# A streaming encoder step in one scheduled stream: first queries in ring tiles, gate products by the memory branch, and the end of attention

## The chip, the cores and the metric

One core of one Trainium2 chip runs the whole program. The metric is the device time of one execution in microseconds (us), lower is better. The engines have short names: PE is the matmul engine TensorE, PEld its weight loads, DVE VectorE, ACT ScalarE, POOL GpSimd, and SP the engine whose queue issues the DMAs. Each engine works off its own queue in order and waits at semaphores for the others.

## The reference

One layer of an encoder on 1024 prompt tokens and 64 sample tokens, in fp32. The three branches of the mixer and the three gates come out of one projection:

```python
h = rmsnorm(x, g_mix); p = h @ w_in
qa, ka, va, qi, ki, wi, ub, qm, gates = split(p)
a = dsa_attend(...)        # 8 query heads on 2 kv heads of 64, over keys that an indexer selects per query
b = pool_mix(ub)           # trailing means over 2, 4, 8, 16 tokens, and a linear map per group
m = memory_attend(qm, mk, mv)   # 4 heads of 128, 256 memory tokens
ga, gb, gm = sigmoid(gates)
x = x + (ga * (a @ w_oa) + gb * (b @ w_ob) + gm * (m @ w_om)) @ w_out
y = x + (silu(h2 @ w_gate) * (h2 @ w_up)) @ w_down      # h2 = rmsnorm(x)
```

## The kernel before, in words

Every fp32 product is made of three matmuls of rounded halves, high by high, high by low and low by high (`matmul3`, L118); a half is made by a rounding copy (`whi` by L98 on POOL, `ph` by L799 on ACT) and a subtraction on DVE (`lo_of`, L88). The kernel is one program text that the Tile framework's scheduler turns into one queue per engine, at build time. What sets the order there is the program's data, the tiles' rings (a tile name with a tag and `bufs=n` has n buffers, handed out in the order of the program text, and a later one waits until the buffer's last reader is done) and explicit `issue_after` marks; independent matmuls are drawn between others.

Around the change the work runs in this order. The keys and values are projected token block by token block (L124, `mm<-tmhi,hh`): a block is normed and rotated (L216 on ACT, L127 and L128 on POOL, L220 and L154 to L157 on DVE), the keys are split (`kd`, L592, L593), transposed (L599), copied (L602) and stored to `k_t` in HBM (L603). The memory cross-attention comes next, in two halves of two heads. In each, the memory keys are transposed (L753); for each of eight blocks of 128 tokens the queries are loaded (`qn`, L758), transposed (L761), split (`qh` L779, `ql` L780), multiplied with the keys (`mm<-kh,qh`), softmaxed (maximum L727 on DVE, exponentials L732 on ACT, reciprocal L733, two scalings L735 on POOL), transposed again (L741), split (`ph` L799, `pl` L88), and multiplied with the values for two blocks together (`mm<-ph,vh`), whose result is split into `bh` and `bl` (L810, L88).

Beside this runs `fill_gate(0, side_a[:, 0], 0, 8)`: the eight 128-column blocks of the gate of branch a, f = 0 to 7. Each loads a raw weight tile (`fraw`), splits it into a pair of tiles `whi` and `wlo` (rings of two buffers each), and multiplies it in three chunks of 364, 362 and 362 tokens with the normed input's halves `hh` and `hl`: 72 matmuls with names like `fl<-hh,whi`, a tanh (L247, `fsg`) per chunk and a store (L635). These products need nothing of the branches. After the memory branch stand the products of its result with w_om (`fill_om`, `fl<-bh,whi`), whose ready-made halves are loaded into the same `whi` and `wlo` rings from `w_pre`.

Then the queries of attention's first block are loaded (`q0`, a tile of the ring `raw` of three buffers, which also holds the memory branch's keys and values), split (`qs0`, L870 and L871), transposed (L883) and copied (`qT_first`, L884). Attention works off blocks of 128 queries in the order `BLOCKS = (2, 7, 1, 6, 0, 8, 5, 4, 3)`, for two key heads each: logits (L1053), mask and maximum (L1065), exponentials (L1067), reciprocal (L1069), scalings (L1071, four on POOL), transposes (L1085), split into `ph` (L1089) and `pl` (L88), value products (L1093), then the result's parts (L1098 to L1102) and its halves (L1111, L1112). The values are split once by `split_values` (L1014, L1015). The last step (block 3, key head 1) has nothing after it but the merge: `merge` (L1150 and following) multiplies the result with w_oa, and L1159 and L1160 combine it with the gate on DVE. Four merges of the first 384 tokens stand in the attention's end (`tr<-bh,whi`); the loop after it takes all other chunks (`mm<-bh,whi`, 352 wide).

## Time and profile before

| | us |
|---|---|
| median of 3 runs | 1708.93 (1707.88 to 1710.14) |
| the profiled execution | 1706.33 |
| its span on the core | 1704.6 |
| PE busy | 1678.4 |
| DVE busy | 1136.4 |
| ACT busy | 808.3 |
| POOL busy | 410.2 |
| DMA, mean | 169 GB/s |

The profiled execution's own time is 1.7 us longer than its span. Busy times are sums over instructions; for PE, matmuls overlap and their ends are modelled, so a busy PE isn't PE at its peak. A wait in the profile names the instruction that released the waiting one. The granted clock is a share of TensorE's full speed.

### The profile page before, as it was taken

The page shows a single profiled execution, that of the slowest core. Times are in us where ns is not written, and L with a number is a line of the kernel's source. Part 1 is how long each engine was busy: PE and PEld are TensorE (multiplying, and loading weights), DVE is VectorE, ACT ScalarE, POOL GpSimd, SP SyncE. Part 2 cuts the span into 40 slices and gives each one's busy share as a digit, 9 for nine tenths or more (in the row PEclk, how much of TensorE's full clock was granted, in tenths as well). Part 3 has the DMA queues.
Part 4 walks back from the last instruction along what each step waited for, and adds up shares of the span by engine and source line. Part 5 has one row for each costly group of instructions (what it writes and reads, how often), then busy time and mean ns, then how long its engine had stood idle before and what let it go on. Part 6 is the DMA issues. An engine that isn't in the chain of part 4 may idle for free.

```text
span 1704.6 us, 32578 instructions
## 1 busy us (share of the span) xinstructions
PE 1678.4 (98%) x12037; PEld 1635.4 (96%) x12037; DVE 1136.4 (67%) x2552; ACT 808.3 (47%) x1942; POOL 410.2 (24%) x480
## 2 busy tenths in 40 slices
PE   9999999999999997999999999999999999999999
PEld 8999999999999997889898999999999999999999
DVE  7578999999973433767673676667657565575543
ACT  5456667755723444776532443334334333353331
POOL 4212424434431223553403431111111000000000
PEclk9999999999999999999999999999999999999999
DMA  6455851234365237435677634554535443596761
GB/s 226 135 181 204 280 158 47 73 129 146 118 217 162 87 102 243 127 119 170 215 266 257 196 117 133 195 195 149 188 113 182 146 170 103 177 368 220 213 189 54
DMA packets 158383, 288.61 MB, mean 169 GB/s; under 512 B 18184, under 2 KB 95872, under 8 KB 158224
## 3 DMA queue, kind: packets, MB, share of 16 engines
q1 hardware_dynamic: 158224, 286.53, 50.6%
q8 instruction: 95, 1.56, 0.4%
q14 instruction: 64, 0.52, 0.1%
HBM read 194.60 MB, written 91.87 MB: 168 GB/s over the span
## 4 chain that ended last, share of the span: by engine, by line
PE 55%; DVE 1%; ACT 1%; issue 0%; POOL 0%; DVEq 0%; ACTq 0%
PE mm L1370 25%; PE mm L1597 14%; PE mm L124 11%; PE fl L124 2%; PE acc L1093 1%; PE tr L1053 1%; PE mm L1085 1%; DVE pl L88 0%; POOL pr L1071 0%; ACT pr L1067 0%; ACT ph L1089 0%; PE mm L1308 0%; DVE pr L1065 0%; PE tr L124 0%; PE tr L1031 0%
## 5 line engine op out<-in xcount | busy, mean ns | idle before, releaser
L1370 PE MATMUL mm<-hi,whi 128*128 128x288 f32 (+1 forms) x1120 | 322.9, 289 | 1.1 <-ACT whi L1362 1.1
L1370 PE MATMUL mm<-lo,whi 128*128 128x288 f32 (+1 forms) x1120 | 323.4, 289 | 0.0
L1370 PE MATMUL mm<-hi,wlo 128*128 128x288 f32 (+1 forms) x1120 | 323.3, 290 | 0.0
L1370 PEld LDWEIGHTS mm<-hi,whi 128*128 128x128 f32 x1120 | 211.8, 189 | 1.6 <-ACT whi L1362 1.6
L1370 PEld LDWEIGHTS mm<-lo,whi 128*128 128x128 f32 x1120 | 211.7, 189 | 0.0
L1370 PEld LDWEIGHTS mm<-hi,wlo 128*128 128x128 f32 x1120 | 211.0, 189 | 0.0
L124 PE MATMUL fl<-hh,whi 128*128 128x362 f32 (+1 forms) x528 | 174.5, 330 | 0.0
L124 PE MATMUL fl<-hl,whi 128*128 128x362 f32 (+1 forms) x528 | 174.3, 330 | 0.0
L124 PE MATMUL fl<-hh,wlo 128*128 128x362 f32 (+1 forms) x528 | 173.8, 329 | 0.0
L1597 PE MATMUL mm<-ul,wh 128*128 128x256 f32 (+1 forms) x600 | 171.7, 288 | 0.0
L1597 PE MATMUL mm<-uh,wh 128*128 128x256 f32 (+1 forms) x600 | 171.1, 288 | 0.0
L1597 PE MATMUL mm<-uh,wl 128*128 128x256 f32 (+1 forms) x600 | 170.3, 288 | 0.0
L921 ACT ACTIVATE junk_a<-score,cand_a,sgn_a 128x512 f16<-128x512 f32 (+2 forms) x93 | 95.5, 1027 | 45.8 <-DVE cand_a L938 21.1
L1597 PEld LDWEIGHTS mm<-ul,wh 128*128 128x128 f32 x600 | 112.7, 188 | 0.0
L1597 PEld LDWEIGHTS mm<-uh,wh 128*128 128x128 f32 x600 | 112.4, 188 | 0.0
L1597 PEld LDWEIGHTS mm<-uh,wl 128*128 128x128 f32 x600 | 112.2, 188 | 0.0
L124 PEld LDWEIGHTS fl<-hh,whi 128*128 128x128 f32 x528 | 99.3, 188 | 0.7
L124 PEld LDWEIGHTS fl<-hh,wlo 128*128 128x128 f32 x528 | 99.3, 188 | 0.6
L124 PEld LDWEIGHTS fl<-hl,whi 128*128 128x128 f32 x528 | 99.3, 188 | 0.4
L88 DVE TENSOR_TENSOR wl<-raw,wh 128x512 fp32r<-128x512 f32 x75 | 51.8, 690 | 70.6 <-ACT wh L1587 70.5
L924 DVE TENSOR_SCALAR_CACHE_REDUCE junk_v<-score,cand_v 64x192 f16<-64x192 f32 (+1 forms) x124 | 93.9, 757 | 2.6
L1587 ACT CAST wh<-raw 128x512 fp32r<-128x512 f32 x75 | 46.6, 621 | 101.1 <-PE mm L1597 97.8
(447 smaller groups left out, 4638.3 us busy)
## 6 DMA issues: line engine op xcount, KB each, us to landing
uf<-u SPq DMA_DIRECT2D x75, 272.0 KB, 4.1
raw<-in_w_up_dram SPq DMA_DIRECT2D x26, 512.0 KB, 3.9
fraw<-in_w_gates_dram SPq DMA_DIRECT2D x23, 512.0 KB, 4.1
fr<-in_w_gate_dram SPq DMA_DIRECT2D x22, 512.0 KB, 4.0
dr<-in_w_down_dram SPq DMA_DIRECT2D x22, 512.0 KB, 6.0
s<-dr SPq DMA_DIRECT2D x22, 512.0 KB, 2.9
raw<-s SPq DMA_DIRECT2D x44, 256.0 KB, 4.0
whi<-w_pre SPq DMA_DIRECT2D x20, 512.0 KB, 4.0
```

What stands on the lines that cost most here:

```text
L88: return V.tensor_tensor(lo, src, hi.bitcast(F32), op=OP.subtract)
L124: PE.matmul(ps, l, r, start=i == 0, stop=i == len(prods) - 1)
L921: A.activation(junk[:n, :nk], sc, AF.Sign, bias=bj, scale=1.0 if scale is None else scale[:n, j:j + 1], accum_out=sj)
L924: V.tensor_scalar(junk[:n, :nk], sc, bj, None, op0=OP.is_ge, op1=OP.add, accum_out=sj)
L1053: lm = PE.matmul(lg[:n, i * 512:i * 512 + cn], qT[:, h, :n], kT[:, kv, s, k0 + c:k0 + c + cn], start=s == 0, stop=s == 1)
L1085: t_ = PE.transpose(pt[:cn, i * n:(i + 1) * n], probs[i][:, c:c + cn], ident[:n, :n])
L1093: m_ = PE.matmul(acc, vv, r, start=ji == 0 and i == 0, stop=ji == nj - 1 and i == 1)
L1370: PE.matmul(dst[i], l, r, start=start and j == 0, stop=stop and j == 11, skip_group_check=True)
L1587: A.copy(wh, raw)
L1597: PE.matmul(acc[f, i], l[:, fs], r[:, cs], start=start and j == 0, stop=stop and j == 2, skip_group_check=True)
```

## The change

It makes these edits:

1. The first queries' code (load, split, transposes, copies) moves in the text from behind `fill_gate(0, ...)` to ahead of it. `qT_first` takes a buffer of the ring `raw`, and `qs0` one of the ring `whi`, where both had a pool of their own.
2. `matmul3` returns its last matmul. For the last gate block (f = 7) the second and third chunk are issued after the memory branch's last value product. `split_values` is issued after the last copy into `qT_first`.
3. In the last softmax (block 3, key head 1) DVE doubles the sums, and ACT takes the scalings of every second head, so that POOL has two and not four.
4. The halves of the last block's first key head are made with POOL and no longer with DVE (L1112).
5. For the third and fourth merge in attention's end, DVE's two operations are issued after the last `pl`.
6. The merge loop's first block takes the tokens from 736 ahead of those from 384.

```diff
-    def fill_gate(base, dst, f0=0, f1=KT):
+    def fill_gate(base, dst, f0=0, f1=KT, last=None):
         for f in range(f0, f1):
             w = fgate(base + f)
             for c0, cn in CH:
-                SP.dma_start(dst[f, :, c0:c0 + cn], fsig(w, c0, cn))
+                with tc.issue_after(last) if last and f == f1 - 1 and c0 else nullcontext():
+                    sg = fsig(w, c0, cn)
+                SP.dma_start(dst[f, :, c0:c0 + cn], sg)
...
-    rest = [(f, ci) for f in range(KT) for ci in (1, 0)]
-    fill_gate(0, side_a[:, 0], 0, 8)
-    for _ in range(1):
-        fill_om(*rest.pop(0))
...
-    early_c = tc.tile_pool(name="early", bufs=1)
-    early = early_c.__enter__()
-    qT_first = early.tile([128, HA, 128], F32R, name="qT0")
+    qT_first = wp.tile([128, 1024], F32R, name="qT0", tag="raw", bufs=3).rearrange("p (h t) -> p h t", h=HA)
     q0 = raw_tile()[:, :512].rearrange("p (h d) -> p h d", h=HA)
     SP.dma_start(q0.rearrange("p h d -> p (h d)"), q_a[TS[BLOCKS[0]][0]:TS[BLOCKS[0]][0] + 128])
-    qs0 = early.tile([128, HA, 2, HDA], F32R, name="qs0")
+    qs0 = wl.tile([128, 1024], F32R, name="qs0", tag="whi", bufs=2).rearrange("p (h s d) -> p h s d", h=HA, s=2)
...
-        A.copy(qT_first[:, g:g + 4], ps.rearrange("p (h t) -> p h t", h=4))
+        qt_copy = A.copy(qT_first[:, g:g + 4], ps.rearrange("p (h t) -> p h t", h=4)).ins
+
+    rest = [(f, ci) for f in range(KT) for ci in (1, 0)]
+    fill_gate(0, side_a[:, 0], 0, 8, mem_mm[0])
+    for _ in range(1):
+        fill_om(*rest.pop(0))
...
+                end = (b, kv) == (BLOCKS[-1], 1)
+                if end:
+                    V.tensor_scalar(sm, sm, 2.0, None, op0=OP.mult)
                 V.reciprocal(sm, sm)
                 for j, pr in enumerate(probs):
-                    G.tensor_scalar(pr, pr, sm[:, j:j + 1], 0.5, op0=OP.mult, op1=OP.mult)
+                    if end and j % 2:
+                        A.activation(pr, pr, AF.Copy, scale=sm[:, j:j + 1])
+                    else:
+                        G.tensor_scalar(pr, pr, sm[:, j:j + 1], 1.0 if end else 0.5, op0=OP.mult, op1=OP.mult)
...
-                    halves_of(av, cs, t0, n, V if b == BLOCKS[-1] else G)
+                    halves_of(av, cs, t0, n, V if (b, kv) == (BLOCKS[-1], 1) else G)
...
                 if not todo:
-                    split_values()
+                    with tc.issue_after(qt_copy):
+                        split_values()
...
-        V.scalar_tensor_tensor(gt, gt, 1.0, ps, op0=OP.add, op1=OP.mult)
-        V.tensor_tensor(pin, pin, gt, op=OP.add)
+        with tc.issue_after(last_pl[0]) if after and f > 1 else nullcontext():
+            V.scalar_tensor_tensor(gt, gt, 1.0, ps, op0=OP.add, op1=OP.mult)
+            V.tensor_tensor(pin, pin, gt, op=OP.add)
...
-        for c0, cn in ACH[1:]:
+        for c0, cn in ACH[1:] if f else ACH[:0:-1]:
```

The order of the instructions shows what the scheduler makes of it. On PE, where the key projection ends and the memory branch begins (`kd` are the split keys, `raw` the memory keys, `qn` the branch's queries), before:

```order
L124 MATMUL fl<-hh,whi 128x364
L599 MATMUL mm<-ident_r,kd 128x64
L753 MATMUL mm<-ident,raw 128x128 x2
L599 MATMUL mm<-ident_r,kd 128x64 x3
L753 MATMUL mm<-ident,raw 128x128 x2
L124 MATMUL fl<-hl,whi 128x364
L124 MATMUL fl<-hh,wlo 128x364
L124 MATMUL fl<-hh,whi 128x362
```

And in the changed program, from the last projection matmul to the first logits (`mm<-kh,qh`; its line numbers are 1 to 4 higher):

```order
L124 MATMUL mm<-tmhi,hl 64x256
L600 MATMUL mm<-ident_r,kd 128x128 x4
L600 MATMUL mm<-ident_r,kd 128x64
L757 MATMUL mm<-ident,raw 128x128 x4
L600 MATMUL mm<-ident_r,kd 128x64 x3
L765 MATMUL mm<-ident,qn 128x128 x4
L124 MATMUL mm<-kh,qh 128x256
L124 MATMUL mm<-kl,qh 128x256
L757 MATMUL mm<-ident,raw 128x128 x4
```

Before, 42 gate matmuls stand between the last two blocks' key transposes, and 46 between L753 and the first query transposes (L761). Now no gate product of f = 0 to 7 stands in the key projection or in the branch's first half: the first of them follows 196 matmuls after the first query transpose, in the second half. Those of f = 0 and 1 are spread over the second half, and those of f = 2 to 7, with the last of f = 1, stand in one piece of 426 behind the branch's last value product. The query transposes of attention's first block (L883, now L873) stand shortly ahead of that piece, and before they stood behind all gate products. From the second `fill_om` product on, PE's order is the same up to the end of attention.

On SP, in the second half of the memory branch, the load of attention's first queries (`raw<-q_a`) and what stands around it, before (`fraw` is a gate's raw weights, `fsg` a gate's result):

```order
L747 DMA raw<-in_cache_mem_k_dram 128x2x256
L635 DMA side_a<-fsg 128x364
L635 DMA side_a<-fsg 128x362 x2
L749 DMA raw<-in_cache_mem_v_dram 128x2x256
L758 DMA qn<-q_m 128x256
L113 DMA fraw<-in_w_gates_dram 128x1024
L758 DMA qn<-q_m 64x256
L635 DMA side_a<-fsg 128x364
L877 DMA raw<-q_a 128x512
```

And in the changed program:

```order
L751 DMA raw<-in_cache_mem_k_dram 128x2x256
L753 DMA raw<-in_cache_mem_v_dram 128x2x256
L762 DMA qn<-q_m 128x256
L762 DMA qn<-q_m 64x256
L762 DMA qn<-q_m 128x256
L867 DMA raw<-q_a 128x512
L762 DMA qn<-q_m 128x256 x2
L113 DMA fraw<-in_w_gates_dram 128x1024
L762 DMA qn<-q_m 128x256
L638 DMA side_a<-fsg 128x364
```

The load of the first queries keeps its place behind the second half's memory tiles, since it takes a buffer of their ring. The tile `qs0` now precedes the gates in the ring of `whi`, and the gates' weight loads and stores have moved behind it.

On DVE, at the end of attention (`pl` are the low halves of the probabilities, `gt<-gt,tr` the merges of the first 384 tokens, `bl<-ot,bh` the last block's low halves), before:

```order
L88 TENSOR_TENSOR pl<-mm,ph 128x512
L88 TENSOR_TENSOR pl<-fl,ph 128x512
L1112 TENSOR_TENSOR bl<-ot,bh 128x2x128
L1159 SCALAR_TENSOR_TENSOR gt<-gt,tr 128x384
L1160 TENSOR_TENSOR gt<-gt 128x384
L88 TENSOR_TENSOR pl<-mm,ph 128x512
L1233 MEMSET ones 128x128
L1101 TENSOR_TENSOR ot<-acc,ot 64x256
```

And in the changed program:

```order
L88 TENSOR_TENSOR pl<-mm,ph 128x512
L88 TENSOR_TENSOR pl<-fl,ph 128x512
L88 TENSOR_TENSOR pl<-mm,ph 128x512
L1168 SCALAR_TENSOR_TENSOR gt<-gt,tr 128x384
L1169 TENSOR_TENSOR gt<-gt 128x384
L1242 MEMSET ones 128x128
L1109 TENSOR_TENSOR ot<-acc,ot 64x256
```

The last three low halves now follow each other, with the third merge's two operations behind them; L1112 of the first key head has left DVE.

## The prediction

> **What bounds the kernel now.** I read four views: the busy table of the page, the waits of TensorE (PE), the windows that cut the span into stretches, and the timeline. The busy table says that there is almost nothing to win on PE's side:

> ```profile
> PE 1678.4 (98%) x12037; PEld 1635.4 (96%) x12037; DVE 1136.4 (67%) x2552; ACT 808.3 (47%) x1942; POOL 410.2 (24%) x480
> ```

> PE is idle for 1704.6 - 1678.4 = 26.2 us in all, and every matmul of the program is still there after the change. So an edit can gain only what PE waits, and loses as much as PE newly waits. The change touches two places. In the first, from the key and value projection to the first attention logits, the waits of PE (480 to 660 us: us in total, times, longest) are:

> ```profile
> PE fl L124 <- ACT qT L884: 4.2, 1, 4.2
> PE mm L883 <- DVE qs L871: 2.1, 1, 2.1
> PE mm L599 <- ACT kd L592: 0.5, 1, 0.5
> ```

> The windows (columns: width, busy us with instructions of PE, PEld, DVE, ACT, POOL, then granted clock, DMA share, GB/s) show the same place from the projection's end to the first queries:

> ```profile
> 518.00:526.00 8.00, 8.00 (x57) 8.00 (x55) 3.13 (x7) 2.22 (x9) 1.93 (x3) 1.00 0.34 100
> 526.00:534.00 8.00, 8.00 (x50) 7.52 (x50) 1.19 (x3) 2.33 (x5) 0.00 (x0) 1.00 0.59 173
> 560.00:600.00 40.00, 40.00 (x279) 39.70 (x278) 17.57 (x35) 17.64 (x48) 6.76 (x12) 1.00 0.29 93
> 600.00:640.00 40.00, 40.00 (x269) 38.74 (x268) 15.09 (x35) 16.67 (x51) 8.58 (x15) 1.00 0.29 92
> ...
> 650.00:655.00 5.00, 2.91 (x23) 2.55 (x22) 2.70 (x5) 1.10 (x2) 1.01 (x1) 1.00 0.59 187
> 655.00:660.00 5.00, 0.82 (x6) 0.68 (x5) 0.00 (x0) 3.39 (x11) 3.39 (x7) 0.73 0.98 327
> 660.00:665.00 5.00, 5.00 (x19) 5.00 (x19) 0.56 (x1) 0.00 (x0) 2.23 (x4) 0.59 1.06 382
> 665.00:670.00 5.00, 5.00 (x31) 5.00 (x30) 1.58 (x4) 0.71 (x2) 2.57 (x3) 1.00 0.70 230
> ```

> Two things are to be seen. Around 655 us PE stands still while the first queries are split, transposed and copied, and behind it the clock is low. But from 518 to 640 us, where short chains run over four engines, PE is never idle. What keeps it busy there are the gate products (`fl<-hh,whi`), long runs of matmuls that wait for nothing; the order of the changed program takes them away from exactly there, because the first queries' tile now stands ahead of them in the ring of two `whi` tiles, and its load stands behind the raw tiles of the memory branch's second half.

> **The change part by part. First queries, gain.** The two waits go, since the gate products of f=2 to 7 now stand behind the query transposes: 4.2 + 2.1 = 6.3 us. The low clock behind them goes too: 31 matmuls in 665 to 670 against 19 in 660 to 665, 12 fewer at 5.00 / 31 = 0.16 us, 1.9 us. What is late next is the weight pair of the first product behind the gates:

> ```profile
> whi<-w_pre SPq DMA_DIRECT2D x20, 512.0 KB, 4.0
> ```

> Its load stands on SP between the stores of the last gate's second and third chunk, so only one chunk of 24 matmuls (24 x 0.16 = 3.9 us) and not all of the tanh, store and 4.0 us of landing is covered: I take 0.9 us of new wait (0 to 2.5). Gain 6.3 + 1.9 - 0.9 = 7.3 us (5.7 to 8.2). ACT's and POOL's splitting of the values (L1014, L1015) moves behind the gates' tanh, but the chain to the first scaled probabilities is longer than it; I cost it at nothing, and the rivals have its price. On SP, the gates' stores and weight loads go from between the branch's loads to behind them, and the value loads (`vf`) stand behind the last gate's stores. That the last gate's last two products wait for the branch's last values costs nothing: their whole group now stands behind it anyway.

> **Lost cover, projection of keys and values.** Timeline rows, one block's last projection matmul and the end of its chain (squares, norm, rotary, split `kd`), then the last block's:

> ```profile
> 502.26 0.28 PE L124 MATMUL mm<-tmhi,hl 128*128 128x256 f32 x1
> 506.10 0.33 PE L124 MATMUL mm<-tmhi,hh 128*128 128x256 f32 x1
> 506.18 0.42 DVE L593 TENSOR_TENSOR kd<-qr,kd 128x256 fp32r<-128x256 f32 x1 [0.47 <-ACT kd L592]
> 509.18 0.28 PE L124 MATMUL mm<-tmhi,hl 128*128 128x256 f32 x1
> ...
> 519.84 0.28 PE L124 MATMUL mm<-tmhi,hl 128*64 128x256 f32 x1
> 519.96 0.46 PE L599 MATMUL mm<-ident_r,kd 128*128 128x128 f32 x4
> 523.75 1.05 POOL L98 TENSOR_SCALAR whi<-fraw 128x1024 fp32r<-128x1024 f32 x1 [1.46 <-PE fl L124]
> 523.99 1.08 DVE L593 TENSOR_TENSOR kd<-qr,kd 64x256 fp32r<-64x256 f32 x1 [0.47 <-ACT kd L592]
> ```

> The chain takes 506.60 - 502.54 = 4.1 us. Now only the next block's 24 matmuls lie over it, 509.46 - 506.10 less the transposes' 0.46 = 2.9 us, so a block can be short by 1.2; but a wait gives the following chain a head start, so that two neighbours together are short of at least 4.1 - 2.9 - 0.46 = 0.7 and at most twice that: between 0.35 and 0.75 a block, 0.55 for some four blocks, 2.2 us (0.5 to 4). The last block has no successor: 525.07 - 520.12 = 4.95, less 0.46 of transposes, is 4.5. In it the split took 1.08 us on half the rows beside POOL's gate split, against 0.42 on its own; that gate split is gone, so I take 4.95 - 0.66 - 0.46 = 3.8 (2.5 to 4.5).

> [...]

> **Lost cover, start of the memory branch.** Timeline rows, the branch's wait on SP's queue (526 to 536 us), and the line view of the query load:

> ```profile
> 528.31 0.44 PE L753 MATMUL mm<-ident,raw 128*128 128x128 f32 x2
> 529.26 0.56 SPq L603 DMA_DIRECT2D k_t<-kt  x1
> 532.18 0.80 SPq L758 DMA_DIRECT2D qn<-q_m  x2
> 536.68 0.86 ACT L779 ACTIVATE qh<-mm,gqm_c 128x256 fp32r<-128x256 f32 x2 [2.81 <-PE mm L761]
> 537.19 0.88 DVE L780 SCALAR_TENSOR_TENSOR ql<-mm,gqm_c,qh 128x256 fp32r<-128x256 f32 x2 [2.89 <-ACT qh L779]
> ```
> ```profile
> SPq L758 <- DMA k_t<-kt: 1.6, 1, 1.6
> ```
> ```profile
> DMA to landing us min/median/max: 2.0/2.5/5.1
> ```

> The first queries of the branch cannot be loaded until the last key store has landed, and the store comes after the last transposes. From PE's last transpose, 528.75, to the second load's issue, 532.98, and its landing at 2.5 are 6.7 us; 46 gate matmuls filled them before, and nothing does now. Less the 0.2 by which the store is earlier without gate traffic ahead, 6.5 us (5.5 to 7.5). Then the queries' split into `qh` and `ql`, each half of its pair's 0.86 and 0.88, lies bare before the first logits: 0.9 us (0.5 to 1.5).

> **Lost cover, the branch's first half.** Timeline rows of one chunk (128 tokens, two heads), then two rows of the lines grouped by form:

> ```profile
> 540.96 0.28 PE L124 MATMUL mm<-kl,qh 128*128 128x256 f32 x1
> 541.08 0.28 PE L124 MATMUL mm<-kh,ql 128*128 128x256 f32 x1
> ...
> 544.07 0.94 POOL L735 TENSOR_SCALAR ex<-ex,sm 128x256 f32<-128x256 f32 x2 [5.57 <-DVE mx L728]
> ```
> ```profile
> L88 DVE TENSOR_TENSOR pl<-mm,ph 128x512 fp32r<-128x512 f32 x16 | 10.9, 689 | 1.9 <-ACT ph L799 1.9
> ...
> L799 ACT CAST ph<-mm 128x512 fp32r<-128x512 f32 x16 | 9.2, 588 | 8.5 <-PE mm L741 8.5
> ```

> From a chunk's last logit (541.36) to its scaled probabilities (545.01) are 3.65 us. PE has two later chunks' logits ahead of the transposes, 12 x 0.12, and 0.5 of query transposes: 1.9. So the first chunk waits 1.7. From then on the value products lie in between, but they wait for `ph` and `pl`, 0.588 + 0.689 = 1.3, with about 0.3 of transposes over it: 1.0 for each of four pairs, 4.0. For queues on ACT and DVE I add 0.3 a pair: together 7 us (4, the value waits alone, to 13, if each of eight chunks waits 1.7). In the second half the gates of f=0 and 1 are back: 1 us (0 to 2).

> **Clock.** After 4.2 us of wait the clock was 0.59 and cost 1.9 us; after 6.5 us I take 2 (0.5, as PE waits there anyway, to 3.8 for two such spells).

> Loss: 2.2 + 3.8 + 6.5 + 0.9 + 7 + 1 + 2 = 23.4 us (13.5 to 36).

> **End of attention.** Waits (826 to 860 us), then timeline rows:

> ```profile
> PE acc L1093 <- DVE pl L88: 1.1, 2, 0.9
> PE mm L124 <- DVE gt L1159: 0.7, 1, 0.7
> ```
> ```profile
> 836.20 3.22 POOL L1071 TENSOR_SCALAR pr<-pr,sm 128x512 f32<-128x512 f32 x4 [0.54 <-DVE sm L1069]
> ...
> 850.12 0.42 DVE L1112 TENSOR_TENSOR bl<-ot,bh 128x256 fp32r<-128x256 f32 x1
> 850.45 0.55 DVE L1159 SCALAR_TENSOR_TENSOR gt<-gt,tr 128x384 f32<-128x384 f32 x1
> 851.03 0.56 DVE L1160 TENSOR_TENSOR gt<-gt 128x384 f32<-128x384 f32 x1
> ```

> The three DVE operations from 850.12 to 851.59 now stand behind the last `pl` (the first of them goes to POOL for the half before, where nothing waits for it), so its wait of 0.9 goes. Of the 0.7 before the first 128x352 product I expect half, 0.4: a tail chunk comes first, which must still wait for its buffers. Splitting POOL's four scalings of 3.22 us between two engines brings the first value products forward, but an added doubling and merge operations stand ahead of the reciprocal; 0.3. Gain 1.6 us (0 to 2.3).

> **Sum.** 23.4 - 7.3 - 1.6 = +14.5 us. The profiled execution took 1706.33 us, its span 1704.6 and 1.7 around it; it becomes 1720.8. It lay 2.6 below the median of the three runs, 1708.93; on the median's scale the forecast is 1723.4. With all bounds together the sum runs from +3 to +31.

> **The rivals.** *The cover was not needed (faster).* If the chains of the two stages are so much shorter without the gates' DVE, ACT and POOL work beside them that PE's waits there stay under 8.9 us, the gains win. Place: from the last `kd` transposes to the first gate product; it decides at the first query transpose of the branch. For it: the two gate-split rows above show that these engines slow each other. Against: the store, the landing and the 4.1 us chain don't depend on gates, and make 6.5 + 3.8 = 10.3 us already. At its price of no loss, 1708.9 - 8.9 = 1700.0. Chance 0.06.

> *The branch keeps pace.* The first half waits only 1 us, the clock 0.5: 15.9 of loss, +7.0, 1715.9. For it: each engine's own share in 560 to 600 is under half (17.6 of 40). Against: the single chain. Chance 0.14.

> *The clock stays down.* If each gap in the first half pulls the clock back, its 196 matmuls before the first gate product take 0.24 instead of 0.12 us: 23.5 more, of which the 8 us of waits absorb a part: some 15 in place of 2, 1736. For it: the 0.59 above. Against: at half speed PE has no gaps left, and the 12 slow matmuls ended by themselves. Chance 0.08. [...]

> *The front gain isn't had.* The change doesn't do what it says if PE stops behind the gates for the late weights or the values' split: the 6.3 come back, 1729.7. Chance 0.07.

> **How the numbers follow.** The forecast has 0.65. Its own range by its bounds, rarely all on one side, is 1714 to 1734. The range 1712 to 1738 takes in the second and third rival nearly whole and leaves out the first. About 0.2% (3.4 us) is what a measurement of this kernel tells from no change. Faster by more: 0.06, the first rival. Within: 0.05, the low end of the second. Slower: 0.89.

> **What would show it.** Right: PE's waits grow by a wait of about 6.5 us at the first query transpose of the branch (`qn`), one of 3 to 4 at `kd` transposes, and many of about 1 at `ph`, `pl` and `ex`; the waits for `qT` and `qs` go; gate products run in one block at PE's pace; PE's busy share falls to about 97.5%. The last `pl` starts right behind the one before. Wrong: PE full between the projection and the first gate product, or a wait of over 3 us at the first attention logits.

## The result, and the profile after

The changed kernel takes 1733.79 us (median of 4 runs, 1733.14 to 1734.15), the kernel before in the same comparison 1708.41 (1706.42 to 1710.14): a ratio of 1.0149, 95% interval 1.0131 to 1.0166, or 25.4 us slower. The forecast was slower by 14.5, 1723.4, with a range up to 1738.

The profiled execution took 1734.15 us. Its span and busy times:

```profile
span 1732.4 us, 32597 instructions
...
PE 1689.2 (98%) x12037; PEld 1642.0 (95%) x12037; DVE 1133.4 (65%) x2552; ACT 810.1 (47%) x1944; POOL 409.8 (24%) x479
```

The span is 27.8 us longer than before. PE's idle time went from 26.2 to 1732.4 - 1689.2 = 43.2 us, 17.0 more. The same 12037 matmuls were busy 10.8 us longer. So there are two parts, waits and slower matmuls, and they add up to the whole.

The waits of PE between 480 and 700 us (us in total, times, longest). Before, the same work ended at 674 us, with four rows, 7.6 us in all: the prediction's three and 0.8 at the first attention logits. Now there are 24.6 us, 17.0 more:

```profile
PE mm L765 <- DMA qn<-q_m: 10.9, 5, 6.5
PE mm L600 <- ACT kd L593: 5.8, 4, 3.1
PE mm L124 <- ACT ph L803: 4.2, 4, 1.6
PE tr L1055 <- DVE mx L1067: 1.1, 1, 1.1
PE mm L124 <- DVE sm L737: 1.0, 1, 1.0
PE mm L745 <- POOL ex L739: 0.9, 1, 0.9
PE fl L124 <- DVE gt L698: 0.7, 1, 0.7
```

The two waits at the first queries, 4.2 and 2.1, are gone. In their place stand the waits for `kd`, for the memory branch's queries `qn`, and for `ph`: the chains that the gate products used to lie over. The timeline at the start of the memory branch, PE and SP rows:

```profile
517.83 0.41 PE L600 MATMUL mm<-ident_r,kd 64*128 64x64 f32 x3
...
518.67 0.55 SPq L604 DMA_DIRECT2D k_t<-kt  x1
521.77 0.81 SPq L762 DMA_DIRECT2D qn<-q_m  x2
...
524.72 1.49 PE L765 MATMUL mm<-ident,qn 128*128 128x128 f32 x4 [6.48 <-DMA qn<-q_m]
525.41 1.30 SPq L762 DMA_DIRECT2D qn<-q_m  x2
...
530.25 0.69 PE L765 MATMUL mm<-ident,qn 128*128 128x128 f32 x2 [1.80 <-DMA qn<-q_m]
...
531.16 0.41 PE L124 MATMUL mm<-kh,ql 128*128 128x256 f32 x1
531.38 0.41 PE L124 MATMUL mm<-kh,qh 128*128 128x256 f32 x1
```

The chain is the one that was forecast: key transposes, key store, its landing, query load, its landing, 6.5 us with PE empty. The last two rows show the second part: the branch's logits now start 0.22 us apart, and before 0.12. PE's later waits in the branch, whose first half ends at 560 us:

```profile
538.45 0.38 PE L124 MATMUL mm<-ph,vh 128*128 128x256 f32 x1 [0.97 <-DVE sm L737]
546.16 0.58 PE L124 MATMUL mm<-ph,vh 128*128 128x256 f32 x1 [1.64 <-ACT ph L803]
555.62 0.38 PE L124 MATMUL mm<-ph,vh 128*128 128x256 f32 x1 [0.74 <-ACT ph L803]
559.97 0.38 PE L124 MATMUL mm<-ph,vh 128*128 128x256 f32 x1 [1.22 <-ACT ph L803]
564.40 0.41 PE L765 MATMUL mm<-ident,qn 128*128 128x128 f32 x2 [0.73 <-DMA qn<-q_m]
567.05 0.66 PE L765 MATMUL mm<-ident,qn 128*128 128x128 f32 x2 [1.27 <-DMA qn<-q_m]
571.45 0.44 PE L745 MATMUL mm<-ident,ex 128*128 128x128 f32 x2 [0.92 <-POOL ex L739]
591.46 0.39 PE L124 MATMUL mm<-ph,vh 128*128 128x256 f32 x1 [0.64 <-ACT ph L803]
```

The windows (columns as before the prediction's windows) give the granted clock; their edges are laid where it changes:

```profile
512.00:515.42 3.42, 1.90 (x17) 1.57 (x15) 0.96 (x5) 1.98 (x7) 0.87 (x2) 1.00 0.35 102
515.42:518.83 3.41, 1.18 (x8) 0.86 (x8) 1.50 (x6) 1.03 (x3) 0.00 (x0) 1.00 0.54 146
518.83:522.24 3.41, 0.00 (x0) 0.00 (x0) 0.00 (x0) 0.05 (x1) 0.00 (x0) 0.51 0.48 115
...
532.48:535.90 3.42, 2.83 (x15) 2.71 (x14) 1.83 (x5) 1.75 (x6) 0.00 (x0) 0.50 0.24 81
535.90:539.31 3.41, 2.44 (x17) 1.84 (x16) 2.64 (x8) 3.08 (x10) 1.66 (x4) 0.99 0.12 38
...
542.72:546.14 3.42, 1.76 (x12) 1.19 (x10) 2.88 (x9) 3.35 (x11) 1.07 (x3) 1.00 0.13 41
546.14:549.55 3.41, 3.39 (x15) 3.05 (x16) 0.86 (x2) 1.28 (x5) 1.51 (x4) 0.51 0.00 0
549.55:552.96 3.41, 3.41 (x19) 3.41 (x17) 1.77 (x3) 1.32 (x3) 0.21 (x1) 0.50 0.11 38
552.96:556.38 3.42, 2.53 (x19) 2.07 (x18) 2.69 (x7) 2.79 (x11) 0.76 (x2) 0.99 0.38 114
...
771.42:774.83 3.41, 2.24 (x18) 1.67 (x16) 2.55 (x8) 2.59 (x9) 1.14 (x4) 1.00 0.65 202
774.83:778.25 3.42, 3.42 (x15) 2.94 (x15) 0.48 (x3) 1.99 (x5) 2.33 (x5) 0.51 0.21 70
```

The clock is at half from 518.8 to 535.9, from 546.1 to 553.0, from 566.6 to 570.0, and once more, far behind, at 774.8: 30.7 us. Before it was at half once, for 6.8 us. How long PE was busy in the longest spell now, and in the one before:

```profile
518.90:535.95 17.05, 8.70 (x37) 7.52 (x38) 5.87 (x14) 5.89 (x16) 0.94 (x2) 0.50 0.61 182
```
```profile
657.30:664.15 6.85, 4.58 (x14) 4.58 (x15) 0.28 (x1) 2.21 (x8) 4.44 (x9) 0.51 1.06 385
```

At the end of attention, the last value product starts without its wait of 0.90, right behind its `pl`:

```profile
879.51 0.69 DVE L88 TENSOR_TENSOR pl<-mm,ph 128x512 fp32r<-128x512 f32 x1 [0.77 <-ACT ph L1097]
...
880.26 0.50 PE L1101 MATMUL acc<-pl,vb 128*128 128x512 f32 x1
```

### The profile page after: what moved, and what is told of

The parts are those of the page before. It is cut to its first block, busy times and chain, and to the rows that moved or that the text cites. A ratio compares the mean times of both kernels' runs of the same rounds, so it can differ in the third digit from the quotient of the medians.

```text
span 1732.4 us, 32597 instructions
## 1 busy us (share of the span) xinstructions
PE 1689.2 (98%) x12037; PEld 1642.0 (95%) x12037; DVE 1133.4 (65%) x2552; ACT 810.1 (47%) x1944; POOL 409.8 (24%) x479
## 4 chain that ended last, share of the span: by engine, by line
PE 66%; DMA 3%; ACT 2%; DVE 1%; issue 1%; POOL 0%; SPq 0%; DVEq 0%; ACTq 0%; POOLq 0%
PE mm L1379 25%; PE mm L1606 13%; PE mm L124 13%; PE fl L124 8%; PE acc L1101 2%; PE tr L1055 2%; PE mm L1093 2%; DMA qn<-q_m 1%; DMA gt<-side_m 1%; PE mm L745 0%; DVE pl L88 0%; DMA raw<-mem_v 0%; PE mm L765 0%; DMA side_a<-fsg 0%; PE tr L124 0%
## 5 line engine op out<-in xcount | busy, mean ns | idle before, releaser
L124 PE MATMUL fl<-hh,whi 128*128 128x362 f32 (+1 forms) x528 | 174.4, 330 | 0.0
L124 PE MATMUL fl<-hl,whi 128*128 128x362 f32 (+1 forms) x528 | 173.8, 329 | 0.0
L124 PE MATMUL fl<-hh,wlo 128*128 128x362 f32 (+1 forms) x528 | 173.1, 329 | 0.0
L124 PEld LDWEIGHTS fl<-hh,whi 128*128 128x128 f32 x528 | 99.7, 189 | 0.7
L124 PEld LDWEIGHTS fl<-hl,whi 128*128 128x128 f32 x528 | 99.5, 189 | 0.4
L124 PEld LDWEIGHTS fl<-hh,wlo 128*128 128x128 f32 x528 | 99.1, 188 | 0.7
L88 DVE TENSOR_TENSOR wl<-raw,wh 128x512 fp32r<-128x512 f32 x75 | 51.8, 690 | 71.8 <-ACT wh L1596 70.9
L1596 ACT CAST wh<-raw 128x512 fp32r<-128x512 f32 x75 | 46.6, 621 | 102.5 <-PE mm L1606 97.5
## 6 DMA issues: line engine op xcount, KB each, us to landing
raw<-in_w_up_dram SPq DMA_DIRECT2D x26, 512.0 KB, 3.9
fraw<-in_w_gates_dram SPq DMA_DIRECT2D x23, 512.0 KB, 3.8
fr<-in_w_gate_dram SPq DMA_DIRECT2D x22, 512.0 KB, 4.0
dr<-in_w_down_dram SPq DMA_DIRECT2D x22, 512.0 KB, 6.0
s<-dr SPq DMA_DIRECT2D x22, 512.0 KB, 3.0
whi<-w_pre SPq DMA_DIRECT2D x20, 512.0 KB, 4.4
```

The source lines that it names most:

```text
L88: return V.tensor_tensor(lo, src, hi.bitcast(F32), op=OP.subtract)
L124: m_ = PE.matmul(ps, l, r, start=i == 0, stop=i == len(prods) - 1)
L1596: A.copy(wh, raw)
```

## The experiments

The theory to be tested: the loss comes from one thing alone, that the first queries' split tile `qs0` stands ahead of the gates in the ring of `whi` tiles, so that the gate products come too late to cover the key projection and the memory branch. The first rival: the edits at the end of attention, or the added issue marks, cost the time. All ratios are to the kernel before, whose medians on the same chips were 1707.3 to 1707.9.

**The two halves of the change, each alone.** The first kernel is the changed one with the four edits at the end of attention undone; the second is the kernel before with those four edits.

```diff
# front only, on the changed kernel
...
-        for c0, cn in ACH[1:] if f else ACH[:0:-1]:
+        for c0, cn in ACH[1:]:
# end only, on the kernel before
...
-                    halves_of(av, cs, t0, n, V if b == BLOCKS[-1] else G)
+                    halves_of(av, cs, t0, n, V if (b, kv) == (BLOCKS[-1], 1) else G)
...
```

> The changed kernel with the four edits at the end of attention undone. Ring theory (all of the loss comes from the first queries' tile standing ahead of the gates in the ring of whi tiles): the front keeps its whole cost, 26 to 27.5 us by the start of the first value product in the profile after, and the end gives back the 1.1 us that the profile after shows gained between the last softmax and the last value product: 1733.8 + 1.1 = 1735 (1733 to 1737). Rival (the edits at the end cost time, since the last reciprocal stands 0.5 us later in the profile after): below 1733, about 1731.

> The kernel before with the four edits at the end of attention alone. Ring theory: the 1.1 us of gain that the profile after shows there, and nothing else, 1708.4 - 1.1 = 1707.3 (1706 to 1708.5). Rival (the edits at the end cost time): 1710 or more.

Front only: 1732.7 us, ratio 1.0148 (1.0134 to 1.0162). End only: 1706.01 against 1707.58, ratio 0.9989 (0.9980 to 0.9998). The whole loss is in the front. The first median lies 0.3 below the ring theory's span, by the letter on the rival's side; but end only is faster than the kernel before and not slower, which speaks against the rival. The two profiles say what happened in front only: PE is idle for 1730.6 - 1686.1 = 44.5 us, 1.3 more than in the changed kernel, as giving back the end's gain would have it, and busy 3.1 less. In that execution the granted clock was 0.993 and not 0.991, though PE's matmuls run in the same order up to the end of attention. The end is a small gain, as forecast; its waits for `pl` (L88) at the value products went from 1.1 us to:

```profile
PE acc L1099 <- DVE pl L88: 0.4, 2, 0.2
```

**The ring.** One kernel gives `qs0` a buffer of the ring `raw`; nothing else differs from the changed kernel. The other leaves it in `whi` but writes six of the gates ahead of the first queries.

```diff
# raw ring
-    qs0 = wl.tile([128, 1024], F32R, name="qs0", tag="whi", bufs=2).rearrange("p (h s d) -> p h s d", h=HA, s=2)
+    qs0 = wp.tile([128, 1024], F32R, name="qs0", tag="raw", bufs=3).rearrange("p (h s d) -> p h s d", h=HA, s=2)
...
# six gates first
+    fill_gate(0, side_a[:, 0], 0, 6)
     qT_first = wp.tile([128, 1024], F32R, name="qT0", tag="raw", bufs=3).rearrange("p (h t) -> p h t", h=HA)
...
-    fill_gate(0, side_a[:, 0], 0, 8, mem_mm[0])
+    fill_gate(0, side_a[:, 0], 6, 8, mem_mm[0])
```

> The changed kernel with one word different: the first queries' split tile takes a buffer of the ring of raw tiles and not of the ring of whi tiles; the text's order and all other edits stay. Ring theory: as with six gates first, 1700 (1698 to 1703); PE's waits for qn, kd and ph go, and those for qT and qs stay away. Rival (the place in the text and the issue marks make the loss, not the ring): 1730 or more.

> The changed kernel with the gates of f = 0 to 5 written ahead of the first queries and those of f = 6 and 7 behind them. Ring theory: the cover is back for the projection and the branch, the first queries stand ahead of the last gate products all the same, so the losses of 28 us go and the gains stay: 1708.4 - 7.3 (front) - 1.1 (end) = 1700 (1698 to 1703), clock at 1.00 from 480 us to the first logits. Rival (the loss hangs on the first queries' code standing ahead of any gate, and on the added issue marks): 1720 or more.

Raw ring: 1705.33 us, ratio 0.9983 (0.9974 to 0.9993). PE's waits for `qn` are gone, and those for `kd` and `ph` fell from 5.8 and 4.2 us to 1.1 and 1.8. Six gates first: 1701.75 us, ratio 0.9966 (0.9954 to 0.9978). One tag is worth 28 us, so the ring theory stands, and neither the text's place nor the issue marks make the loss. The raw ring misses the expected span by 2 us, and both gain less than the 8.4 that I had put together. PE's waits from 640 to 692 us with six gates first show what is left:

```profile
PE tr L1056 <- DVE mx L1068: 1.7, 2, 1.1
PE tr L1056 <- ACT ph L1098: 1.5, 1, 1.5
PE mm L124 <- ACT ph L803: 1.0, 1, 1.0
PE fl L124 <- DVE gt L698: 0.7, 1, 0.7
PE mm L1094 <- POOL pr L1080: 0.5, 1, 0.5
```

The waits of 4.2 and 2.1 are gone, but 1.5, 1.0 and 0.7 are new. The values land only behind the last gate product, so their splitting runs on ACT between the first row maximum and the first exponential.

**The values' splitting.** On six gates first, it is issued behind the first softmax's last exponential.

```diff
...
-                    with tc.issue_after(qt_copy):
+                    with tc.issue_after(last_ex[0]):
                         split_values()
```

> The kernel with six gates first, and the split of the values issued after the first softmax's last exponential. In the profile with six gates first, the values land only behind the last gate product, and ACT's eight copies of them, 1.9 us from 663.6, stand between the first row maximum (664.1) and the first exponential (667.2); PE then waits 1.5 us for ph at the logits, a wait that the kernel before doesn't have. Theory (this split is where the rest of the front's gain went): that wait goes, 1701.75 - 1.5 = 1700.2 (1699 to 1701.5). Rival (the value products then wait for the split in its place, with POOL's 3.9 us ahead of a scaling): 1702 or more.

1701.89 us, ratio 0.9962 (0.9949 to 0.9974): no gain over six gates first. The wait for `ph` went, and another came at the same logits:

```profile
PE tr L1056 <- ACT qT L1036: 1.6, 1, 1.6
```

The copies of the second block's queries stand on ACT behind the values now. ACT's queue holds the 1.5 us whichever goes first; the rival was near, but with another chain.

**Two gates first.**

```diff
+    fill_gate(0, side_a[:, 0], 0, 2)
...
-    fill_gate(0, side_a[:, 0], 0, 8, mem_mm[0])
+    fill_gate(0, side_a[:, 0], 2, 8, mem_mm[0])
```

> The changed kernel with the gates of f = 0 and 1 written ahead of the first queries and six behind them. Stage theory (each stage's loss comes back only where its own cover is missing): two gates cover the key projection (5.8 us of kd waits) and the branch's start (6.5 us and the clock behind it, some 5), and the branch's first half stays bare: 1733.8 - 5.8 - 6.5 - 5 = 1716.5 (1713 to 1720). Rival (the loss is shared evenly by the gates, 1733.8 with none and 1701.8 with six ahead, 5.3 us each): 1723.

1720.52 us, ratio 1.0080 (1.0066 to 1.0093): between the two, half a microsecond above the stage theory's span. PE's waits (480 to 712 us), the rows for the stages in question:

```profile
PE mm L765 <- DMA qn<-q_m: 6.5, 3, 4.9
PE mm L124 <- ACT ph L803: 4.7, 5, 1.6
...
PE mm L600 <- ACT kd L593: 0.9, 1, 0.9
```

The projection's waits are covered (5.8 to 0.9) and so is the branch's start. But a wait of 4.9 for queries comes later, where the two gates end: the stage theory holds for the projection, and the loads move the rest.

**The old place, in ring tiles.** The first queries' code goes back behind the gates and the first `fill_om`; `qs0` stays in `whi`.

```diff
-    qT_first = wp.tile([128, 1024], F32R, name="qT0", tag="raw", bufs=3).rearrange("p (h t) -> p h t", h=HA)
...
     rest = [(f, ci) for f in range(KT) for ci in (1, 0)]
     fill_gate(0, side_a[:, 0], 0, 8, mem_mm[0])
...
     load_keys(0, 384)
+    qT_first = wp.tile([128, 1024], F32R, name="qT0", tag="raw", bufs=3).rearrange("p (h t) -> p h t", h=HA)
...
```

> The changed kernel with the first queries' code back at its old place in the text, behind the gates and the first product with w_om, but still in the ring tiles. Ring theory: the cover is whole, since the tile now follows the gates in the ring; the query transposes come after 12 matmuls of the first w_om product, and 12 more lie behind them, so part of the two waits of the kernel before stays: 1702 to 1706. Rival (a tile in the ring of whi costs the cover wherever it stands): over 1715.

1705.77 us, ratio 0.9987 (0.9976 to 0.9998). A tile in the gates' ring doesn't cost the cover when it comes after them. Of 6.3 us of waits at the first queries, 0.8 is left (`fl` for `qT`), but the gain of 1.65 is no more than the end's alone: in the profile other waits stand there (1.9 for `pr`, 0.5 before; 1.8 for `ph`, none before), and the clock is at half for 13.6 us, 6.8 before. Its 12 executions run from 1701.98 to 1709.36, though it is one program: three at a granted clock of 1.000 have a mean of 1702.4, two at 0.996 of 1708.7. The four at 0.998 spread from 1704.26 to 1709.07, so the granted clock, as it is listed, doesn't account for all of it. I come back to that below.

**The clock.** Extra matmuls whose result nobody reads are put into the waits: 40 into the 6.5 us wait for the branch's first queries, and then 18 into the 3.1 us wait for the last `kd` and 38 into the 6.5. The second edit:

```diff
...
+            with tc.issue_after(last_kd[4]):
+                pd = fps(362)
+                for i in range(18):
+                    PE.matmul(pd, hh[:, i % KT, :128], hh[:, i % KT, 364:726], start=i == 0, stop=i == 17)
+            with tc.issue_after(last_kd[0]):
+                pd = fps(362)
+                for i in range(38):
+                    PE.matmul(pd, hh[:, i % KT, :128], hh[:, i % KT, 364:726], start=i == 0, stop=i == 38 - 1)
```

> The changed kernel with 40 extra matmuls of 128x362, whose result nobody reads, between the last key transposes and the memory branch's first query transposes, where PE waits 6.5 us in the profile after. 40 x 0.167 = 6.7 us, so they take the wait's place. Clock theory (the half clock behind that wait, 17 us of it with 9 us of busy PE, costs time by itself): clock 1.00 at the first query transposes, 3 to 5 us faster than the changed kernel, 1729 to 1731. Rival (PE waits for the chains there in any case, so the clock costs nothing): 1733 to 1734.

> The changed kernel with 18 extra matmuls of 128x362 in PE's 3.1 us wait for the last kd, and 38 in the 6.5 us wait for the first branch queries (the earlier kernel with 40 in the second wait alone found the clock at half already, and its extra matmuls took 9 us). 18 x 0.167 = 3.0 and 38 x 0.167 = 6.3 us, so at full clock they fit into the waits. Clock theory: clock at 1.00 until the branch's first logits, the first spell of half clock (17 us, 9 us of busy PE in it) gone, 2 to 4.5 us faster than the changed kernel, 1729 to 1732, with PE's busy time less the extra 9.3 us at about 1684 and not 1689. Rival (what the clock gives the chains' waits take): 1733 or more.

40 alone: 1733.72 us, ratio 1.0152 (1.0139 to 1.0166), no change. The clock had fallen already at the `kd` wait, so the extra matmuls ran at half clock until 523.3 us, took 8.7 us and not 6.7, and held the first queries until 527.81 instead of 524.72. What the clock gave behind them was spent ahead of them, so this one decides nothing. Both waits filled: 1732.88 us, ratio 1.0145 (1.0129 to 1.0160), under 1 us better than the changed kernel and between the two expectations. The clock held until 529.7 us, and then:

```profile
527.80 0.28 PE L124 MATMUL mm<-kh,ql 128*128 128x256 f32 x1
531.85 0.69 PE L767 MATMUL mm<-ident,qn 128*128 128x128 f32 x2 [3.77 <-DMA qn<-q_m]
```

PE arrived earlier at the next query load, waited for it, and the clock fell there. The profile shows the exchange. The clock is at half for 13.6 us and not 30.7. PE's busy time, less the 9.3 us of extra matmuls, is 1684.7, 4.5 less than in the changed kernel, as the clock theory had it; but the rest of the span is 46.0 us, 2.8 more. So 1.7 us are left of the 4.5: in this stretch the waits, that for this load first, take most of what the clock gives.

**The query loads.** SP's own waits in the changed kernel (517 to 534 us) say why there are four more waits for queries:

```profile
SPq L762 <- PE mm L765: 4.4, 5, 1.3
```

With two buffers a load is issued only when PE has transposed an earlier tile. One kernel has three, and the last has three and the extra matmuls.

```diff
-                qn = mp.tile([128, 256], F32, name="qn", tag="qn", bufs=2)[:n]
+                qn = mp.tile([128, 256], F32, name="qn", tag="qn", bufs=3)[:n]
...
```

> The changed kernel with three instead of two buffers for the memory branch's query tiles. In the profile after, PE waits four more times, 4.4 us, for a query load in the branch besides the first 6.5. If they come from the two buffers (a load is issued only when a pair has been transposed): 2 to 5 us faster, 1729 to 1732. Rival (the loads are late for the first key store and the queue, or the softmax chain takes the wait's place): 1733 to 1734.

> Both aids at once: the extra matmuls in both waits (alone 1732.9 us) and three buffers for the branch's query tiles (alone 1730.8), on the changed kernel (1733.8). With the extra matmuls alone the clock held until 529 us and PE then waited 3.8 us for the second query load, so the loads took what the clock gave. If clock and loads hide each other, removing both gives more than the sum of 0.9 and 3.0: 1727 to 1729. Rival (the next chain, the scaled probabilities ex and the halves ph, takes their place): 1729.9, the plain sum, or more.

Three buffers: 1730.8 us, ratio 1.0136 (1.0123 to 1.0149), 3.0 less than the changed kernel, in the first theory's span. Of the four further waits for queries one of 0.4 is left, so they did come from the two buffers. But waits of the same size came back, most of them at the scaled probabilities:

```profile
PE mm L765 <- DMA qn<-q_m: 6.3, 2, 5.9
...
PE mm L745 <- POOL ex L739: 3.8, 2, 2.3
```

PE is idle for 1727.6 - 1684.3 = 43.3 us in this profile, and 43.2 in the changed kernel's. What is shorter is its busy time, by 4.9 us, with the clock at half for 17.1 us and not 30.7. So the gain is not the waits that went; as far as one profile of each shows, it is the clock. Whether the clock stayed up because these waits went isn't shown.

With both aids: 1733.31 us, ratio 1.0145 (1.0125 to 1.0164), neither expectation. Its four executions are 1730.84 and 1730.95 at a granted clock of 0.997 and 0.996, and 1735.67 and 1736.35 at 0.994 and 0.993. In the profiled one, at 0.993, the clock is at half from 531 to 545 us, longer than the 518 to 528 us without the extra matmuls. PE waited 3.06 us for a query load there, until 532.04. So extra work in the two long waits didn't keep the clock up in this execution: behind them it fell again.

## Why the prediction was right in kind and short in size

**Right: where the loss comes from.** The order of the changed program said that no gate product covers the projection and the branch's first half, and the ring's tag alone makes and unmakes the loss. The forecast's terms against the profile after: the `kd` waits 2.2 + 3.8 = 6.0, measured 5.8 (2.7 + 3.1); the first query load 6.5, measured 6.48; the first half's waits at its four value products 4.0, measured 1.0 + 1.6 + 0.7 + 1.2 = 4.6. The last block's split of `kd`, 1.08 us beside POOL's gate split before, now takes 0.41 to 0.43 like all nine, as its term assumed. POOL's split beside it took 1.05, the median of its kind (`whi<-fraw`), so that row shows DVE slowed and not POOL. The 0.9 for the queries' own split shows as no wait. The rivals by which the cover was not needed or the branch keeps pace fell with these rows.

**Right in sign, its size by luck: the end of attention.** 1.6 was forecast; end only gave 1707.58 - 1706.01 = 1.6, interval 0.3 to 3.4. Of the sum behind it, the waits for `pl` fell by 0.7 where 0.9 was forecast, and the wait for `gt` ahead of the first 128x352 product, of which 0.4 was to go, is 0.7 in the profiles before and after. Which of the four edits does the rest wasn't tried.

**Failed: the clock term.** "After 6.5 us I take 2" was the step. I took one spell of half clock, as long as the one before, and against the 1.9 us gained it came to nothing. The profile has four spells, 30.7 us, and matmuls that are busy 10.8 us longer. The rival by which the clock stays down, at a chance of 0.08 and with 1736, came nearest, but I argued it down with the thought that at half speed PE has no gaps. It has: during the first spell PE was busy 9 of 17 us. How much of the 10.8 is the clock's own can be estimated from the spells. PE was busy for 22.0 us in the four and for 4.6 in the one before; if that work takes half as long at full clock (the logits stand 0.22 us apart in the first spell, and 0.12 before), the spells account for (22.0 - 4.6) / 2 = 8.7 us. The other profiles bear this out: over the ten kernels without extra matmuls PE's busy time runs from 1675.8 to 1689.2 us, and less half of what lies in spells only from 1675.8 to 1678.9. The executions of one program point to the same size: the kernel before has a mean of 1706.9 over 13 executions at a clock of 0.998 and 1710.2 over 6 at 0.996, 1.65 us per 0.001; the changed kernel's 0.9918 (mean of four) lies 0.0055 under the 22 executions of before (0.9973), which at that rate is 9 us. This is the clock's share of the difference, and not what its repair alone would give back: with both waits filled 4.5 us of busy time went and only 1.7 of the span.

**Too small: the branch's second half.** The first half's 7 us came out, in part by luck: its later waits are 4.6 at the value products and 1.8 + 0.6 for query loads, 7.0 in all. I had made them of softmax chains alone. I had priced the first query load and not the following ones, which with two buffers wait for PE's own transposes: 10.9 - 6.5 = 4.4 us more in both halves. The second half, taken at 1, waits for 0.7 + 1.3 + 0.9 + 0.6 = 3.6 us, 2.0 of it ahead of its first gate product at 568.8.

**Too large: the front's gain.** 7.3 was forecast. With the cover kept, front and end together give 5.8 (six gates first, 1707.58 - 1701.75), so the front some 4.2. The late values were a rival of mine at 6.3; in the profile they stand for a wait of 1.5 at the first logits, which moving them only turned into another, and two waits of 1.0 and 0.7 for `ph` and `gt` behind the branch were missing from the sum.

**What the range owes to luck.** The prediction's own bounds gave 1714 to 1734, and the 1733.8 lies at their very end. Without the clock's two terms the forecast adds up to 14.4, against 17.0 us of added idle time; what fills the rest is the clock, which the sum had at 2 - 1.9, next to nothing.

**The best kernel here** is six gates first, 1701.75 us: it beats the changed kernel by 32 and the kernel before by 5.8 us. It does what the change says, two gates' products behind the branch, without taking the other six there.

## What to carry to other kernels

In a scheduler that hands out ring buffers in the order of the text, a tile that borrows a ring from filler work puts all of that work behind its own inputs; look in the built order for where the filler went, not at the line that moved. Price the cover that goes as the chains it lay over, the loads behind the first one included, and then add the clock: here it was at half for 30.7 us and not 6.8, and in the 3.4 us ahead of its fall at 546.2 no wait was longer than 1.64 us. To judge a few microseconds here, compare executions with their granted clocks: those of the old place spread over 7 us, with a mean of 1702.4 at 1.000 and of 1708.7 at 0.996. And look whether a gain lies in PE's idle time or in its busy time: of the loss here, 17.0 us are the one and 10.8 the other.

## What the runs showed of the hardware

The edges don't stand at the same times in every execution. With the same order of matmuls up to there, the first fall comes at 657.3 us before and at 656.2 in end only; and in front only the logits take 0.41 us up to 536.30 and 0.28 from 537.99 on, while in the profile after the clock is back at 535.9. My estimate from this is that the same short waits can fall into one stretch in one execution and into two in the next, which would account for part of one program's running at 1702 and at 1709 us. That it is the cause was not tried.
